# The delta rule's gates ahead of K's convolution in the program, the logits' copy on ScalarE

## The chip, the cores and the metric

One core of a Trainium2 chip. The metric is the device time of one execution in microseconds, as the median of three runs. The engines are TensorE (PE; its weight loads are PEld), VectorE (DVE), ScalarE (ACT), GpSimd (POOL) and SyncE (SP), which issues all weight transfers.

## The reference, cut to what matters

Two transformer blocks on 256 tokens of width 1024, all in float32. The first block has a mixer of two halves (retention, and a gated delta rule), a router with 32 experts of which each token uses two, and a second block follows with a pooling mixer and a convolutional feed-forward layer. What concerns the change is the delta rule's input:

```python
d_q, d_k, d_v, d_z, d_a, d_b = ...                    # columns of h @ w_in
qkv = silu(causal_dwconv(concat(d_q, d_k, d_v), conv_w))   # four taps per channel
dk = l2norm(heads(ck))
beta = sigmoid(d_b)
g = -exp(a_log) * softplus(d_a + dt_bias)             # log decay, the gate
dn = gated_delta_rule(dq, dk, heads(cv), g, beta)
```

Inside the delta rule the decay between two tokens is the exponential of differences of the running sum of g, and the matrix to be inverted is (beta k) k^T times this decay.

## The kernel before, in words

Activations are kept transposed, [128 channels x 256 tokens] per block of channels. Products in float32 are run as three matmuls on split operands (`split`, lines 281 and 284: ScalarE writes the rounded high part, VectorE or GpSimd subtracts for the low part; `mm3`, line 290: the three matmuls).

The work goes in stages: the modulation vectors from w_ada; normed and modulated input (lines 499 to 506); K's projection (line 509, into four PSUM tiles ps5); K's convolution; the gates; the matrix Am and its inverse in levels of doubling blocks (line 705, tiles Am, Zc, Xc, Q); V's and Q's convolutions; the delta rule's products; retention; the output projection; the router; 16 pairs of experts (lines 1289 and 1317); the tail with the feed-forward layer (line 290 again).

The program's order is only a rank. The framework's planner goes over all stages, and gives each engine, whenever it is free by the planner's own estimates, the ready instruction that stands first in the program. Work of a later stage so fills the waits of an earlier one. On the chip each engine's queue then runs strictly in the planned order. Only the router (TensorE, VectorE) and the experts (TensorE, SyncE) keep the order in which they are written.

The lines that the change and the prediction touch:

- `conv_silu`: line 562 scales a projection by the last tap into y, line 563 copies it raw (both ScalarE, four blocks each); line 568 adds the other three taps on VectorE, three instructions per block; line 571 is the Silu on ScalarE. For K it is called at line 600 with the ready ps5, so it issues no matmul and no DMA.
- the gates, lines 602 to 638: line 605 computes the eight logits (psab), line 608 copies them (abT), line 611 transposes them by two small matmuls, line 613 copies them out (ab). From there small operations on [128 x 8]: beta (615 to 617, an Exp and a reciprocal), xa and na (619 to 622, an Exp), and the softplus as a series on VectorE (625 to 636), up to gg at line 638.
- behind the gates: line 642 (running sum of gg by a matmul), 646 (Exp of it, egc), 651 to 661 (the decay Dm, an Exp), then `sumsq(yk)` (lines 583 to 591) and Am (685 to 689).
- `copy` (lines 205 to 210) and `affine` (lines 212 to 217) share one counter:

```python
def copy(dst, src):
    _alt[0] ^= 1
    if _alt[0]:
        V.tensor_copy(dst, src)
    else:
        S.activation(dst, src, AF.Copy)
```

  The copy of abT is the first call in the program, so it is VectorE's. Later callers are rows of the modulation (g1b, g2b), Q in the inverse, atT, rqT, rkT, rv, reto, the copies xt for the router's logits, and oT and hidT of each pair of experts.

Of the kernel before, what the change touches and what calls it, by code (L numbers as in the profile page):

```python
# [13 lines left out]
AF = mybir.ActivationFunctionType  # L14
# [6 lines left out]
T = 256  # L21
# [158 lines left out]
def build(ctx, tc, io, out, dbg=None):  # L180
    nc = tc.nc
    V, S, G, PE = nc.vector, nc.scalar, nc.gpsimd, nc.tensor
# [8 lines left out]
    def bank(tag=None):  # L191
        return pp.tile([128, 512], F32, name="ps", tag=tag or ptag[0])
# [12 lines left out]
# [6 lines that stand above are left out]
# [8 lines left out]
    def dump(name, ap):  # L219
        if dbg is not None and name in dbg:  # L220
            nc.gpsimd.dma_start(dbg[name], ap)
# [40 lines left out]
    def ft(shape, name, bufs=None, tag=None, dtype=F32):  # L262
        return fp.tile(shape, dtype, name=name, tag=tag or name, **({"bufs": bufs} if bufs else {}))

    def t4(shape, name):
        return dp.tile(shape, F32, name=name, tag="t4", bufs=N4)
# [20 lines left out]
    def mm3(ps, ah, al, bh, bl, first, last):  # L287

        for n, (a, b) in enumerate(((ah, bh), (ah, bl), (al, bh))):
            PE.matmul(ps, lhsT=a, rhs=b, start=first and n == 0, stop=last and n == 2)  # L290
# [194 lines left out]
    ps5 = [bank("pb")[:, :T] for m in range(4)]  # L485
# [43 lines left out]
    def hp(part, k, t=None):  # L529
        a = hs_[k // 4][part][:, k % 4, :]  # L530
        return a if t is None else a[:, 128 * t:128 * t + 128]
# [14 lines left out]
    def conv_silu(w, off, ps=None, first=()):  # L546

        first = list(first)
        if ps is None:
            ps = [bank("pb").rearrange("p (i t) -> p i t", i=2) for m in range(2)]  # L550
            for m in range(4):
                for k4 in range(2):
                    wh, wl = first.pop(0) if first else next(w)
                    for kk in range(4):
                        k = 4 * k4 + kk
                        mm3(ps[m // 2][:, m % 2, :], wh[:, kk, :], wl[:, kk, :], hp(0, k), hp(1, k), k == 0, k == 7)
            ps = [ps[m // 2][:, m % 2, :] for m in range(4)]
        y = t4([128, 4, T], "y")
        raw = t4([128, 4, T], "raw")
        for m in range(4):  # L560
            c = 4 * (off + m)
            S.activation(y[:, m, :], ps[m], AF.Copy, scale=convw[:, c + 3:c + 4])
            S.activation(raw[:, m, :], ps[m], AF.Copy)
        for m in range(4):
            c = 4 * (off + m)
            for tap in range(3):
                sh = 3 - tap
                V.scalar_tensor_tensor(
                    y[:, m, sh:], raw[:, m, :T - sh], convw[:, c + tap:c + tap + 1], y[:, m, sh:],
                    op0=ALU.mult, op1=ALU.add)  # L570
            S.activation(y[:, m, :], y[:, m, :], AF.Silu)
        return y
# [24 lines left out]
        G.tensor_tensor(r, x, mhalf[:, :, None].to_broadcast([128, 2, 4]), op=ALU.pow)  # L597
        return r

    yk = conv_silu(None, 4, ps5)  # L600

    psab = bank()
    for kk in range(2):
# [1 line left out]
            PE.matmul(psab[32 * q:32 * q + 32, :T], lhsT=wab[:, 2 * q + kk, :], rhs=hT(2 * q + kk),  # L605
                      start=kk == 0, stop=kk == 1)
    abT = dp.tile([128, T], F32, name="abT")
    copy(abT, psab[:, :T])
    psab2 = bank()
    for t in range(2):  # L610
        PE.matmul(psab2[:, 8 * t:8 * t + 8], lhsT=abT[:, 128 * t:128 * t + 128], rhs=cfv("sel32"), start=True, stop=True)
# [24 lines left out]
    V.scalar_tensor_tensor(xa, xa, 0.0, lnu, op0=ALU.max, op1=ALU.add)  # L636
    gg = ft([128, 2, 4], "gg")
    V.scalar_tensor_tensor(gg, xa, -1.0, ea, op0=ALU.mult, op1=ALU.mult)
    dump("gg", gg)
    dump("beta", beta)  # L640
    psg = bank()
# [899 lines left out]
```

## Time and profile before

| | us |
|---|---|
| median of three runs | 890.74 (889.5 to 893.18) |
| the profiled execution | 890.27 |
| its span, first to last instruction | 888.5 |
| TensorE busy in the span | 842.7 (95%) |
| VectorE busy | 401.4 (45%) |
| ScalarE busy | 272.4 (31%) |
| GpSimd busy | 153.1 (17%) |
| DMA, mean over the span | 288.54 MB, 325 GB/s |

Busy times are shares of the whole span, over stages with different limits; a busy TensorE may run at either level of its clock, which the granted clock shows (1.00 is full speed). In a timeline, the bracket at the end of a line is the idle time of the engine just before it and what ended it.

### The profile page before, as it was taken

What the parts mean: (1) busy time and instruction counts of PE and PEld (TensorE: products, weight loads), DVE (VectorE), ACT (ScalarE), POOL (GpSimd) and SP (SyncE); (2) the same over time, 40 slices, a digit from 0 to 9 for tenths busy, and PEclk for the clock granted to TensorE, in tenths of its full rate; (3) what the DMA queues carried; (4) which work ended last, traced back from release to release, by engine and by line L of the source; (5) the groups of instructions that cost most, each with busy time, mean ns of one, the idle gap of its engine ahead of it and who ended that gap; (6) DMA issues with size and microseconds to landing.
All of it is one profiled execution on the core that took longest, in us unless ns stands there. A gap on an engine that the chain in (4) does not pass through costs nothing.

```text
span 888.5 us, 12970 instructions
## 1 busy us (share of the span) xinstructions
PE 842.7 (95%) x5337; PEld 534.7 (60%) x5337; DVE 401.4 (45%) x757; ACT 272.4 (31%) x512; POOL 153.1 (17%) x115
## 2 busy tenths in 40 slices
PE   2988999989989999999999998998999999999998
PEld 0675778768734435343343532544435999898996
DVE  3577587586611222212122211232214977667664
ACT  2253244364501101010010100101104665555552
POOL 0234331162000000000000001021000033533525
PEclk9998999999999999999999999999999999999999
DMA  9982779767589999999999999999999955453001
GB/s 379 423 360 97 285 281 378 290 252 315 190 327 377 423 428 426 429 427 427 428 427 426 429 427 426 429 428 426 421 409 426 409 202 190 182 198 142 1 2 47
DMA packets 26113, 288.54 MB, mean 325 GB/s; under 512 B 3009, under 2 KB 3265, under 8 KB 9793
## 3 DMA queue, kind: packets, MB, share of 16 engines
q1 hardware_dynamic: 26048, 287.66, 78.6%
q8 instruction: 44, 0.72, 0.3%
q14 instruction: 21, 0.16, 0.1%
HBM read 286.60 MB, written 1.05 MB: 324 GB/s over the span
## 4 chain that ended last, share of the span: by engine, by line
PE 59%; DMA 11%; DVE 1%; issue 0%; ACT 0%; SPq 0%; DVEq 0%; ACTq 0%
PE ps L290 21%; PE ps L1289 20%; PE ps L1317 10%; DMA wt<-in_w 9%; PE ps L1225 3%; PE ps L1248 3%; DMA wt<-in_ffn_w_in 2%; PE ps L1305 1%; PE ps L1237 1%; PE ps L1235 0%; DVE x L1524 0%; DVE x L1425 0%; PE ps L1055 0%; DVE wl L284 0%; DVE hid L1298 0%
## 5 line engine op out<-in xcount | busy, mean ns | idle before, releaser
L1289 PE MATMUL ps<-wt,x 128*64 128x512 f32 x1024 | 228.3, 598 | 6.9 <-DMA wt<-in_w 5.7
L1289 PEld LDWEIGHTS ps<-wt,x 128*64 128x64 f32 x1024 | 75.2, 138 | 151.4 <-issue 134.0
L281 ACT ACTIVATE wh<-wt 128x512 fp32r<-128x512 f32 (+1 forms) x138 | 113.4, 832 | 91.1 <-PE ps L290 82.4
L1317 PE MATMUL ps<-wt,hidT 128*64 128x512 f32 x512 | 115.6, 602 | 2.9 <-issue 1.6
L284 POOL TENSOR_TENSOR wl<-wt,wh 128x512 fp32r<-128x512 f32 (+1 forms) x52 | 94.7, 1833 | 90.1 <-ACT wh L281 87.6
L1298 DVE SCALAR_TENSOR_TENSOR hid<-ps,gs,hid 128x512 f32<-128x512 f32 x16 | 12.0, 752 | 200.0 <-PE ps L1289 200.0
L290 PE MATMUL ps<-gh,wh 128*128 128x256 f32 x352 | 98.5, 280 | 0.2 <-DVE gl L1442 0.2
L290 PE MATMUL ps<-gl,wh 128*128 128x256 f32 x352 | 98.3, 280 | 0.0
L290 PE MATMUL ps<-gh,wl 128*128 128x256 f32 x352 | 98.2, 279 | 0.0
L284 DVE TENSOR_TENSOR wl<-wt,wh 128x1024 fp32r<-128x1024 f32 (+1 forms) x86 | 83.8, 987 | 31.8 <-ACT wh L281 31.6
L1317 PEld LDWEIGHTS ps<-wt,hidT 128*64 128x64 f32 x512 | 38.8, 138 | 66.6 <-issue 64.3
L1053 POOL TENSOR_TENSOR dg<-ca,csh 128x512 fp32r<-128x512 f32 x6 | 6.2, 1040 | 391.1 <-DVE csl L284 320.9
L290 PEld LDWEIGHTS ps<-gh,wh 128*128 128x128 f32 x352 | 66.0, 188 | 0.6 <-ACT gh L1440 0.4
L290 PEld LDWEIGHTS ps<-gh,wl 128*128 128x128 f32 x352 | 66.1, 188 | 0.0
L290 PEld LDWEIGHTS ps<-gl,wh 128*128 128x128 f32 x352 | 65.9, 187 | 0.2
L1328 ACT ACTIVATE Yh<-ps 128x512 fp32r<-128x512 f32 x30 | 17.9, 597 | 109.0 <-DVE ps L1326 64.3
L1326 DVE TENSOR_TENSOR ps<-ps,g2b 128x512 f32<-128x512 f32 x30 | 21.0, 700 | 60.0 <-PE ps L1317 60.0
L1499 POOL TENSOR_TENSOR yf<-yf 128x256 f32<-128x256 f32 x22 | 19.5, 886 | 164.2 <-PE ps L290 95.5
L1494 DVE SCALAR_TENSOR_TENSOR yf<-ps,sm,yf 128x254 f32<-128x254 f32 x88 | 42.0, 479 | 11.2 <-ACT yf L1491 10.0
L1294 ACT ACTIVATE hid<-ps 128x512 f32<-128x512 f32 x16 | 9.6, 597 | 107.1 <-PE ps L1289 107.1
L217 ACT ACTIVATE x<-ps,modT,A 128x256 f32<-128x256 f32 x32 | 17.8, 564 | 70.2 <-PE ps L1225 70.2
L290 PE MATMUL ps<-wh,hfl 128*128 128x512 f32 x88 | 34.7, 394 | 0.0
(388 smaller groups left out, 1268.0 us busy)
## 6 DMA issues: line engine op xcount, KB each, us to landing
wt<-in_w SPq DMA_DIRECT2D x86, 2048.0 KB, 22.1
wt<-in_w_ada SPq DMA_DIRECT2D x12, 2048.0 KB, 13.3
wt<-in_ffn_w_in SPq DMA_DIRECT2D x11, 2048.0 KB, 7.9
wt<-in_w SPq DMA_DIRECT2D x40, 512.0 KB, 10.2
wt<-in_w_in SPq DMA_DIRECT2D x7, 2048.0 KB, 13.9
wt<-in_ffn_w_out SPq DMA_DIRECT2D x5, 2048.0 KB, 8.4
wt<-in_w_out SPq DMA_DIRECT2D x2, 2048.0 KB, 7.9
wt<-in_w_in SPq DMA_DIRECT2D x2, 1024.0 KB, 19.4
```

Of the source, the lines that this page charges most:

```text
L217: S.activation(dst, src, AF.Identity, scale=a, bias=b)
L281: S.activation(hi, src, AF.Copy)
L284: (eng or V).tensor_tensor(lo, src, hi.bitcast(F32), op=ALU.subtract)
L290: PE.matmul(ps, lhsT=a, rhs=b, start=first and n == 0, stop=last and n == 2)
L1225: PE.matmul(ps[d - d % 2][:, d % 2, :], lhsT=x[:, t, 128 * d:128 * d + 128], rhs=OH[:, t].rearrange("p g s -> p (g s)"), start=t == d % 2 ...
L1248: PE.matmul(res[t, c], lhsT=oT[:, 128 * t:128 * t + 128], rhs=y, start=False, stop=False)
L1289: PE.matmul(ps[64 * g:64 * g + 64, :], lhsT=xg[:, k, 128 * (p % 2) + 64 * g:128 * (p % 2) + 64 * g + 64], rhs=wt[p, nm, g][:, k, :], start ...
L1317: PE.matmul(py[c][64 * g:64 * g + 64, :], lhsT=hidT[:, f, 64 * g:64 * g + 64], rhs=wt[p, "w2", g][:, f, 512 * c:512 * c + 512], start=f == ...
L1326: V.tensor_tensor(py[c], py[c], g2c, op=ALU.mult)
L1328: S.activation(yh, py[c], AF.Copy)
L1494: V.scalar_tensor_tensor(y[:, sh:], ps[:, :T - sh], cw[:, 3 * m + tap:3 * m + tap + 1], y[:, sh:], op0=ALU.mult, op1=ALU.add)
L1499: G.tensor_tensor(ys[0], ys[0], ys[1], op=ALU.mult)
```

## The change

The call of K's convolution moves from ahead of the gates to behind gg, and the copy of the logits, until now a call of the alternating helper, is written as a ScalarE activation. The helper's counter is therefore advanced once less, and every later call of `copy` and `affine` takes the other engine.

```diff
-    yk = conv_silu(None, 4, ps5)
 
     psab = bank()
...
     abT = dp.tile([128, T], F32, name="abT")
-    copy(abT, psab[:, :T])
+    S.activation(abT, psab[:, :T], AF.Copy)
     psab2 = bank()
...
     V.scalar_tensor_tensor(gg, xa, -1.0, ea, op0=ALU.mult, op1=ALU.mult)
+    yk = conv_silu(None, 4, ps5)
     dump("gg", gg)
```

## Rows read from the trace of the kernel before

**Rows 1.** Stretches of the span: us of stretch, busy us (instructions) by engine, granted clock, DMA share, GB/s

```profile
60.00:80.00 20.00, 18.11 (x343) 12.04 (x343) 17.96 (x44) 9.25 (x20) 9.60 (x9) 0.91 0.34 119
...
140.00:160.00 20.00, 19.95 (x92) 16.18 (x91) 13.75 (x25) 9.36 (x15) 4.04 (x4) 1.00 1.00 412
...
285.00:645.00 360.00, 352.47 (x1740) 156.19 (x1738) 84.74 (x153) 46.18 (x84) 12.55 (x12) 1.00 1.01 427
```

**Rows 2.** Chain that ended last: start us, us, what

```profile
250.79 7.09 PE ps L1289 x32
...
501.76 7.04 PE ps L1317 x32
...
508.80 36.71 DMA wt<-in_w
```

**Rows 3.** TensorE in order of time, 46 to 73 us: start, us, instruction, [idle before, releaser]

```profile
46.02 1.06 PE L605 MATMUL ps<-hT,wab 128*32 128x256 f32 x14
...
53.17 0.61 PE L611 MATMUL ps<-cf,abT 128*128 128x8 f32 x4 [2.06 <-DVE abT L208]
...
61.09 0.36 PE L642 MATMUL ps<-gg,cf 128*128 128x8 f32 x2 [0.56 <-DVE gg L638]
...
72.21 0.44 PE L705 MATMUL ps<-Zc,Am 32*32 32x16 f32 x32 [0.78 <-DVE Zc L723]
```

**Rows 4.** Stretches, line 290 (V's and Q's convolution matmuls) on TensorE alone

```profile
47.00:51.00 4.00, 3.98 (x32) 1.00 1.04 442
...
53.50:57.30 3.80, 3.66 (x18) 0.55 0.98 418
```

**Rows 5.** VectorE in order of time, 46 to 67 us

```profile
46.69 0.48 DVE L568 SCALAR_TENSOR_TENSOR y<-raw,sm,y 128x254 f32<-128x254 f32 x1
...
49.46 1.53 DVE L568 SCALAR_TENSOR_TENSOR y<-raw,sm,y 128x253 f32<-128x253 f32 x1
...
52.71 0.41 DVE L208 COPY abT<-ps 128x256 f32<-128x256 f32 x1
...
56.32 1.23 DVE L629 TENSOR_TENSOR z<-z 128x8 f32<-128x8 f32 x1
...
60.78 0.17 DVE L638 SCALAR_TENSOR_TENSOR gg<-xa,ea 128x8 f32<-128x8 f32 x1
...
66.11 0.17 DVE L591 TENSOR_SCALAR kk<-ps 128x8 f32<-128x8 f32 x1 [0.85 <-PE ps L588]
```

**Rows 6.** ScalarE in order of time, 47 to 62 us

```profile
47.06 0.43 ACT L563 ACTIVATE raw<-ps 128x256 f32<-128x256 f32 x1
...
48.06 0.42 ACT L571 ACTIVATE y<-y 128x256 f32<-128x256 f32 x1 [0.57 <-DVE y L568]
...
54.04 1.28 ACT L615 ACT_TABLE_LOAD   x1
...
55.33 0.21 ACT L615 ACTIVATE beta<-ab 128x8 f32<-128x8 f32 x1
...
61.78 0.21 ACT L646 ACTIVATE egc<-gc 128x8 f32<-128x8 f32 x1 [4.07 <-DVE gc L644]
```

**Rows 7.** GpSimd in order of time

```profile
49.40 1.30 POOL L284 TENSOR_TENSOR wl<-wt,wh 128x512 fp32r<-128x512 f32 x1 [3.03 <-ACT wh L281]
...
56.24 1.29 POOL L284 TENSOR_TENSOR wl<-wt,wh 128x512 fp32r<-128x512 f32 x1 [4.13 <-ACT wh L281]
```

**Rows 8.** Router, before the experts, 230 to 233 us, all engines

```profile
230.91 1.28 ACT L247 ACT_TABLE_LOAD   x1
...
230.94 0.69 DVE L208 COPY xt<-ps 128x512 f32<-128x512 f32 x1 [0.81 <-PE ps L1002]
...
232.20 0.29 ACT L247 ACTIVATE ss<-ss,ca 128x2 f32<-128x2 f32 x1
```

**Rows 9.** Copies by the alternating helper, lines 208 and 210: duration ns min/median/max

```profile
L208 DVE COPY hidT<-ps x16: 691/692/692, 261.0 to 668.1; 128x512 f32<-128x512 f32 x16
...
L210 ACT ACTIVATE oT<-ps x16: 383/383/384, 258.6 to 644.2; 128x256 fp32r<-128x256 f32 x16
```

## The prediction

> **What bounds the kernel now.** I read the stretches of the span first. From 285 to 645 us the DMA engines are full (share 1.01, 427 GB/s) [rows 1]: the experts' weights set the pace there, and the chain of waits agrees, since it runs over the experts' matmuls and then over weight transfers [rows 2]. That stretch can't be shortened by compute; it can only begin earlier. It begins when the stages ahead of it have released the weight buffers: from 60 to 80 us the DMA share is 0.34 [rows 1], because transfers wait for buffers. So a microsecond won before 250 us moves the experts, and then the tail, by about a microsecond.
>
> Before 250 us TensorE is the scarce engine: busy 19.95 us of 20 from 140 to 160, 18.11 from 60 to 80 [rows 1]. Its queue is in order and is filled by a plan that works on all stages at once: V's convolution matmuls, which stand far behind the gates in the program, run between the gates' small matmuls [rows 3, 4]. Hence the measure of this stage is not the chain of the gates alone, but how long TensorE stands or runs slowly in it. Three rows show that: it waits 2.06 us for abT and 0.56 us for gg, and 0.78 us for Zc in the first levels of the triangular inverse [rows 3]. After the first of these the granted clock drops: 18 matmuls of line 290 start in a stretch of 3.80 us at clock 0.55, where 32 start in 4.00 us at 1.00 [rows 4]. A matmul at full clock thus takes 4.00 / 32 = 0.125 us, 18 would take 2.25, and the loss is 1.55 us.
>
> Why abT is late: the logits are complete at 47.08 (46.02 + 1.06) [rows 3], but the copy is at 52.71 on VectorE [rows 5], behind eleven of K's twelve taps. A tap takes 0.48 us, but 1.53 where GpSimd is at a split's subtraction [rows 5, 7]. Why gg is late: a table load of 1.28 us ahead of the first Exp [rows 6], and one operation on eight columns that takes 1.23 us beside GpSimd [rows 5, 7], where its like takes 0.17 [rows 5].
>
> **The change part by part.** *The copy on ScalarE.* Its queue is free of K's eight copies at 47.49 (47.06 + 0.43) [rows 6]. A ScalarE copy of this shape takes 0.38 us [rows 9], so abT is there at 47.87 instead of 53.12 (52.71 + 0.41 [rows 5]), 5.25 us earlier. TensorE no longer waits for it: minus 2.06 us, and the slow stretch behind that wait goes with it, minus 1.55.
>
> *The gates ahead of the convolution.* Nothing is added or removed. The convolution issues no DMA and nothing on GpSimd or SyncE; eight ScalarE copies, twelve taps and four Silus are moved behind gg. Its first copies are ready before the logits, so they still begin first. What changes is rank: where a tap and a gate operation are both ready, the gate operation goes first, and taps fill the gate chain's waits, which they do at no cost as long as VectorE has waits to fill. Behind the waiting gate operations on VectorE stand the remaining taps, and for these wait K's Silus, the squares and the sums of squares; the sums are read by VectorE at 66.11 now [rows 5].
>
> *The new wait.* The plan now puts the matmul of gg earlier into TensorE's queue, and whatever makes gg late against the plan becomes a wait there, with V's matmuls queued behind it. The present wait of 0.56 is only what remains after TensorE itself had been slowed by 1.55, so gg is about 2.11 us late against the plan. The same two causes give 1.28 for the table load and 1.23 minus 0.17 = 1.06 for the collision: 2.34 us. That is the wait I put at gg, in place of 0.56. Its bounds: 0 if the taps fill it and TensorE has V's matmuls queued in front, and 4.90 if two more table loads get into the chain (2.34 + 2 x 1.28). I take 2.34, being the two rows' own sum. The slow clock after it costs between 0 and 1.55; a wait of 2.06 was followed by it, one of 0.56 was not [rows 3, 4], and I take half, 0.78. The wait for Zc (0.78) has V's matmuls nearly used up ahead of it; with the levels starting earlier more of them remain as filler. Bounds 0 and 0.78; I take it as gone.
>
> *Table loads.* The rows show one load between K's Silus and the gates' Exps [rows 6]. With the gates' Exps ahead of most Silus the queue goes Silu, Exp, Silu, Exp: three loads, two more than now, 2.57 us on ScalarE. ScalarE stands idle 4.07 us before egc [rows 6], which covers them if the Silus do not come between the gates' two Exps. Without that cover each one between them costs 1.28.
>
> Here a rule speaks against the change. The row shows a load of 1.28 us from 54.04 and the next Exp at 55.33 [rows 6], with nothing in between. The Trainium skill (ScalarE: Activation LUTs, What ACT_TABLE_LOAD costs) counts about 2.66 us for each switch of a set, as a drain of about 1.38 goes with the load. By it the wait at gg would be 3.72 and the sum 1.38 us higher than mine; the trace shows no drain, so I keep the row's figure.
>
> *The alternation.* The helper that alternates copies between the two engines is called once less, so every later pair of calls swaps engines. Most swaps cancel (one goes each way). Two do not. hidT goes to ScalarE and oT to VectorE for the experts: 0.69 us against 0.38 for half the width [rows 9], inside a stretch bound by DMA, so nothing. And the last logits' copy ahead of the router (0.69 us on VectorE at 230.94) moves into ScalarE's queue, ahead of the table load that starts at 230.91 and lets the square root run at 232.20 [rows 8]. That adds between 0 and 0.69; I take 0.6, since the root waits for the load there.
>
> The sum: minus 2.06, 0.56, 1.55 and 0.78, plus 2.34, 0.78 and 0.6, is minus 1.2 us. The profiled execution took 890.27 us around its span of 888.5, 0.47 under the median shown; carried to the median, 890.74 - 1.2 = 889.5.
>
> **The rivals.** *The gate chain sets the stage, not TensorE's total.* Then the 5.25 us of abT count, less one switch of 1.28 in front of the Exps, and the 0.85 us that VectorE waits for the sums of squares [rows 5] go too: 5.25 - 1.28 + 0.85 - 0.6 = 4.2 earlier, 886.5. For it: the levels do wait for this chain. Against: TensorE has other work queued almost all the time.
>
> *Exps and Silus take turns, slower.* If a Silu of K gets between the gates' two Exps, the chain to gg holds three loads in place of one; TensorE waits 4.90 instead of 2.34 at gg's matmul and the slow stretch is had in full: plus 2.57 and 0.77 on my sum, 892.8. It decides from the point where the wait at gg exceeds the 4.17 that go now (2.06 + 0.56 + 1.55). For it: the Silu at 48.06 [rows 6] stands right where the first Exp becomes ready. Against: gates now rank first. The Trainium skill (same page, Rules for kernel authors) asks to do all of one set before switching; with its price per switch this case would be 4.1 us later still, 896.9.
>
> *The change doesn't do what it says:* the copy or the gates are still planned behind the taps, or kk2 becomes the last input in place of gg (it is 0.85 late already [rows 5]). Then 890.7.
>
> **How the numbers follow.** I give my forecast 0.42, the chain 0.25, the turns 0.20 and no effect 0.13. The range reaches from the chain's time with no wait at gg to the turns with a swap or two more against it: 885.0 to 894.0. A measurement of this kernel can tell about 0.5% (4.45 us; the three runs span 0.4%). Faster by more needs under 886.3: half of the chain's chance and a little of the forecast's, 0.19. Slower needs over 895.2: a third of the turns' chance, by dearer switches, and some for an unlucky order further on, 0.13. The rest, 0.68, is within.
>
> **What would show it.** Right: abT on ScalarE before 48.5 us, no wait on TensorE at line 611, two to three table loads where there was one, a wait of 2 to 3 us at line 642, gg before 58 us, and the first matmul of line 1289 about a microsecond earlier. The chain is right if the gate matmul waits are gone and the levels begin 4 us earlier with that gain kept at the experts. The turns show as four or more table loads before 62 us and a longer wait at line 642. I am wrong in kind if the difference arises behind 100 us, in the swapped copies or the weight loads.

## The result and the profile after the change

The changed kernel takes 901.74 us (median of four runs, 900.98 to 902.31) against 891.82 for the kernel before in the same session: a ratio of 1.0113, with a 95% interval from 1.0089 to 1.0137. It is slower by some 10 us, outside the forecast's range. Its profiled execution took 902.31 us around a span of 900.5, 12.0 us longer than that of the kernel before.

The chain of waits shows on which side of the experts this arises (start us, us, what):

```profile
262.72 7.09 PE ps L1289 x32
...
520.07 36.98 DMA wt<-in_w
```

The first piece at line 1289 comes 11.9 us later than in [rows 2], so the time is lost ahead of it, and what is lost there is kept to the end. The stretches that answer to [rows 1] agree (the columns are the same):

```profile
60.00:80.00 20.00, 18.17 (x279) 13.26 (x283) 14.81 (x37) 6.61 (x13) 8.19 (x7) 0.76 0.28 105
...
285.00:645.00 360.00, 353.25 (x1741) 152.44 (x1738) 77.61 (x148) 48.06 (x82) 12.09 (x12) 1.00 1.01 427
```

In the experts the pace is the same, 427 GB/s in both. From 60 to 80 us TensorE is as busy as before, but with 279 matmuls in place of 343, at a granted clock of 0.76 where it was 0.91.

TensorE's waits from 44 to 260 us (engine, line, what it waited for: us in total, times, longest) name two places:

```profile
PE ps L642 <- DVE gg L637: 4.8, 1, 4.8
PE ps L976 <- DVE dno L945: 3.0, 1, 3.0
...
PE ps L290 <- DVE wl L284: 1.9, 1, 1.9
PE ps L1016 <- DVE router L1094: 0.9, 1, 0.9
PE ps L705 <- DVE Zc L723: 0.8, 1, 0.8
```

The kernel before has these in their place, beside the waits of [rows 3]:

```profile
PE ps L290 <- DVE wl L284: 2.2, 2, 2.0
...
PE ps L976 <- DVE modT L411: 1.8, 1, 1.8
```

The first place is in the stage that was changed; the second is some 150 us later, in the stage that gates the two branches' outputs, where the diff touches nothing.

*The first place.* TensorE in order of time, the answer to [rows 3] (start, us, instruction, idle before and releaser):

```profile
48.94 0.51 PE L610 MATMUL ps<-cf,abT 128*128 128x8 f32 x4
...
55.37 0.28 PE L290 MATMUL ps<-hh,wh 128*128 128x256 f32 x1
60.49 0.57 PE L642 MATMUL ps<-gg,cf 128*128 128x8 f32 x2 [4.84 <-DVE gg L637]
```

The wait for abT is gone. In its place stands one wait of 4.84 us for gg. (In this execution the logits' matmuls start 0.99 us later than in [rows 3], at 47.01; a shift of this size in the times below says nothing of the change.) ScalarE (to be held against [rows 6]):

```profile
48.13 0.39 ACT L607 ACTIVATE abT<-ps 128x256 f32<-128x256 f32 x1
...
50.77 1.28 ACT L614 ACT_TABLE_LOAD   x1
52.06 0.21 ACT L614 ACTIVATE beta<-ab 128x8 f32<-128x8 f32 x1
...
52.39 1.28 ACT L571 ACT_TABLE_LOAD   x1
53.69 1.03 ACT L571 ACTIVATE y<-y 128x256 f32<-128x256 f32 x3
54.62 1.65 ACT L281 ACTIVATE wh<-wt 128x512 fp32r<-128x512 f32 x3
56.30 1.28 ACT L646 ACT_TABLE_LOAD   x1
```

abT comes from ScalarE at 48.13, as forecast, and there are three table loads, as forecast. But look at what stands behind the second: three Silus, and then three of the splits' high parts (line 281) in a row. No idle time stands in front of them, so what they read was there already, and they stood behind the loads and the Silus in this in-order queue. In the kernel before, the two of this stretch came one by one:

```profile
55.55 0.61 ACT L281 ACTIVATE wh<-wt 128x512 fp32r<-128x512 f32 x1
57.08 0.63 ACT L281 ACTIVATE wh<-wt 128x512 fp32r<-128x512 f32 x1 [0.92 <-PE ps L290]
```

GpSimd makes the low parts from them, and so it gets three at once, where [rows 7] has them apart:

```profile
55.32 3.71 POOL L284 TENSOR_TENSOR wl<-wt,wh 128x512 fp32r<-128x512 f32 x3 [3.00 <-ACT wh L281]
```

VectorE's gate series runs exactly beside it, the answer to [rows 5]:

```profile
49.66 0.17 DVE L612 COPY ab<-ps 128x16 f32<-128x16 f32 x1
...
54.55 4.50 DVE L632 SCALAR_TENSOR_TENSOR lnu<-lnu,z 128x8 f32<-128x8 f32 x7
...
60.17 0.17 DVE L637 SCALAR_TENSOR_TENSOR gg<-xa,ea 128x8 f32<-128x8 f32 x1
...
68.53 0.17 DVE L591 TENSOR_SCALAR kk<-ps 128x8 f32<-128x8 f32 x1 [1.32 <-PE ps L588]
```

The logits' sums are read at 49.66, and still gg is no earlier than 60.17: seven operations on eight columns each take 4.50 us together. What they take undisturbed is shown by e8 below, 1.37. In the kernel before they took 2.35, beside one subtraction on GpSimd:

```profile
57.79 2.35 DVE L633 SCALAR_TENSOR_TENSOR lnu<-lnu,z 128x8 f32<-128x8 f32 x7
```

*The second place* comes up with the experiments that reach it, since it has to be told apart from the first.

*The router*, the answer to [rows 8]: the last copy of the logits now stands on ScalarE, with the table load right behind it.

```profile
242.16 0.60 ACT L210 ACTIVATE xt<-ps 128x512 f32<-128x512 f32 x1
242.78 1.28 ACT L247 ACT_TABLE_LOAD   x1
```

### The profile page after: what moved, and what is told of

Read it like the earlier page. It is cut to its first block, busy times and chain, and to the rows that moved or that the text cites. A ratio compares the mean times of both kernels' runs of the same rounds, so it can differ in the third digit from the quotient of the medians.

```text
span 900.5 us, 12963 instructions
## 1 busy us (share of the span) xinstructions
PE 850.6 (94%) x5337; PEld 535.0 (59%) x5337; DVE 393.6 (44%) x756; ACT 278.3 (31%) x515; POOL 148.8 (17%) x115
## 4 chain that ended last, share of the span: by engine, by line
PE 58%; DMA 11%; DVE 1%; ACT 1%; issue 0%; SPq 0%; DVEq 0%; ACTq 0%
PE ps L290 20%; PE ps L1289 20%; PE ps L1317 10%; DMA wt<-in_w 9%; PE ps L1225 3%; PE ps L1248 3%; DMA wt<-in_ffn_w_in 2%; PE ps L1305 1%; ACT hidT L210 0%; DVE x L1524 0%; PE ps L1237 0%; DVE x L1425 0%; PE ps L1235 0%; PE ps L1055 0%; DVE wl L284 0%
## 5 line engine op out<-in xcount | busy, mean ns | idle before, releaser
L1289 PEld LDWEIGHTS ps<-wt,x 128*64 128x64 f32 x1024 | 73.0, 138 | 154.3 <-issue 135.5
L284 DVE TENSOR_TENSOR wl<-wt,wh 128x1024 fp32r<-128x1024 f32 (+1 forms) x86 | 81.6, 961 | 36.1 <-ACT wh L281 35.8
L1326 DVE TENSOR_TENSOR ps<-ps,g2b 128x512 f32<-128x512 f32 x30 | 21.0, 700 | 60.9 <-PE ps L1317 60.8
L210 ACT ACTIVATE hidT<-ps 128x512 f32<-128x512 f32 x16 | 9.5, 597 | 102.4 <-PE ps L1305 102.4
L382 PE MATMUL ps<-wt,srep 128*32 128x512 f32 x160 | 26.7, 810 | 11.5 <-DMA wt<-in_w_ada 11.5
```

The source lines that it names most:

```text
L284: (eng or V).tensor_tensor(lo, src, hi.bitcast(F32), op=ALU.subtract)
L382: PE.matmul(ps[32 * q:32 * q + 32, :], lhsT=srep[:, 2 * q + kk, :], rhs=w[:, 2 * q + kk, :], start=kk == 0, stop=kk == 1)
L1289: PE.matmul(ps[64 * g:64 * g + 64, :], lhsT=xg[:, k, 128 * (p % 2) + 64 * g:128 * (p % 2) + 64 * g + 64], rhs=wt[p, nm, g][:, k, :], start ...
L1326: V.tensor_tensor(py[c], py[c], g2c, op=ALU.mult)
```

## The experiments

The diff has three effects: the convolution moves behind the gates; the copy of abT goes to ScalarE; and every later copy changes its engine, because the helper's counter advances once less. The first four runs make these one by one. In the table, times are medians, ratios are against the kernel before in the same session, and the events are starts in us in the profiled execution: gg, the first rqT, the second reto, the router's logits. The last column is the distance from the second reto to the router. The events are those of one execution each, and the executions already differ by up to 1.4 us where the logits' matmuls start (45.63 in e8, 47.03 in e10); the ratios decide, the events only show the place.

| kernel | us | ratio (95%) | gg | rqT | reto | router | reto to router |
|---|---|---|---|---|---|---|---|
| before | | 1 | 60.8 | 141.9 | 178.4 | 232.7 | 54.3 |
| after | 901.74 | 1.0113 (1.0089 to 1.0137) | 60.2 | 148.0 | 185.2 | 244.7 | 59.5 |
| e1 | 896.94 | 1.0058 (1.0041 to 1.0075) | 61.3 | 141.9 | 179.1 | 238.0 | 58.9 |
| e2 | 895.22 | 1.0038 (1.0018 to 1.0058) | 59.2 | 146.9 | 183.3 | 238.4 | 55.1 |
| e3 | 895.24 | 1.0038 (1.0024 to 1.0053) | 59.8 | 150.4 | 186.4 | 238.5 | 52.1 |
| e4 | 899.63 | 1.0089 (1.0071 to 1.0106) | 62.7 | 153.6 | 190.6 | 243.3 | 52.7 |
| e5 | 897.05 | 1.0062 (1.0042 to 1.0083) | 59.2 | 146.9 | 184.2 | 239.9 | 55.7 |
| e6 | 893.11 | 1.0028 (1.0013 to 1.0044) | 60.5 | 144.0 | 181.3 | 236.5 | 55.2 |
| e7 | 885.33 | 0.9936 (0.9917 to 0.9956) | 57.2 | 137.4 | 173.9 | 229.0 | 55.1 |
| e8 | 885.64 | 0.9942 (0.9921 to 0.9963) | 57.3 | 138.8 | 175.3 | 228.8 | 53.5 |
| e9 | 886.47 | 0.9948 (0.9922 to 0.9973) | 56.3 | 136.9 | 174.2 | 229.4 | 55.2 |
| e10 | 897.63 | 1.0087 (1.0058 to 1.0117) | 61.7 | 152.2 | 189.3 | 240.9 | 51.6 |

**e1, the swapped copies alone** (edit of the kernel before):

```diff
-    copy(abT, psab[:, :T])
+    V.tensor_copy(abT, psab[:, :T])
```

> Only the alternation is changed: the gates stay behind K's convolution, the logits' copy stays on VectorE, but no longer advances the counter, so every later copy swaps engines as in the changed kernel. Theory G (the loss of some 11 us arises in the gates' stage): within 1 us of the kernel before, first expert matmul after the branch near 251 us. Theory S (the swapped copies further on cost it): 5 us or more slower, with the loss behind 180 us, and both stages up to 100 us as before.

Measured: 1.0058. The swaps that the forecast took for nearly free cost about 5 us. The place is the last column: 58.9 us from reto to the router, 4.6 more than before, and 59.5 in the changed kernel.

**e2, the move and the copy without the swaps** (edit of the changed kernel):

```diff
-    S.activation(abT, psab[:, :T], AF.Copy)
+    S.activation(abT, psab[:, :T], AF.Copy); _alt[0] ^= 1
```

> The whole change, but the counter is advanced once by hand, so that every later copy is on the engine it had before. Theory G: slower than before by 7 to 11 us, with the wait of some 4.8 us for gg and the late levels as in the changed kernel. Theory S: within 2 us of before, or slower by no more than the 2.4 us that the levels begin later in the changed kernel. Both at work: 5 to 7 us slower.

Measured: 1.0038, some 3.4 us, between what theory S allowed (2.4) and the 5 to 7 us expected if both are at work, and the distance from reto to the router is back at 55.1. The loss lies in front: rqT is 5.0 us late. The wait for gg is there in full (4.83 us), and so are the seven operations of 4.50 us. So the change holds two separate losses, and by e1 and e2 they add: 0.0058 + 0.0038 = 0.0096 of the time, inside the interval of the whole change (0.0089 to 0.0137).

**e3, the move alone; e4, the copy alone** (edits of the changed kernel and of the kernel before):

```diff
-    S.activation(abT, psab[:, :T], AF.Copy)
+    copy(abT, psab[:, :T])
```

```diff
-    copy(abT, psab[:, :T])
+    S.activation(abT, psab[:, :T], AF.Copy); _alt[0] ^= 1
```

> Only the move: the gates ahead of K's convolution, the copy on VectorE by the alternating helper as before (no swap later on). Theory G, with the move as the cause: slower by 5 us or more. If instead the copy's engine is what puts gg's matmul too early in TensorE's queue: within 2 us of before. Theory S: within 2 us.

> Only the copy on ScalarE, with the counter advanced by hand (no swap) and the gates still behind K's convolution. Theory G, with the move as the cause: within 2 us of before, or 2 to 3 us faster, since the wait of 2.06 us for abT goes. If the copy's engine is the cause: slower by 3 us or more. Theory S: within 2 us.

Measured: 1.0038 and 1.0089. The move alone costs what the move and the copy cost together, and has the same mark: four subtractions in a row on GpSimd, the seven operations at 4.55 us beside them, and a wait of 4.2 us at line 642. So the engine of the copy isn't what makes gg late in the changed kernel. The copy alone is slower than both together, so the two parts don't add. In e4 a Silu does come between the gates' two Exps, with a table load on either side of it (at 53.37 and 55.10), and VectorE waits for the second Exp:

```profile
56.63 0.17 DVE L625 TENSOR_SCALAR z<-na 128x8 f32<-128x8 f32 x1 [2.81 <-ACT na L622]
```

That is the forecast's rival of the turns, in a kernel for which it was not made; gg is at 62.7 here, the latest of all in the table. But this is the smaller part of the loss of e4; for the rest e10 and e11 were made.

**e5 and e6, one row copy put back.** With the swaps, VectorE's order in the gated stage differs. In e1 (start, us, instruction, idle before):

```profile
189.72 0.69 DVE L944 TENSOR_TENSOR dno<-dno,dsq 128x512 f32<-128x512 f32 x1 [1.75 <-POOL dsq L253]
190.34 2.49 DVE L284 TENSOR_TENSOR wl<-wt,wh 128x512 fp32r<-128x512 f32 x4
```

and in the kernel before:

```profile
188.55 2.49 DVE L284 TENSOR_TENSOR wl<-wt,wh 128x512 fp32r<-128x512 f32 x4
192.57 0.69 DVE L944 TENSOR_TENSOR dno<-dno,dsq 128x512 f32<-128x512 f32 x1 [1.53 <-POOL dsq L253]
```

A product of the delta rule's norm, which has to wait for GpSimd's power, has got ahead of the four subtractions for which TensorE's last gated projection waits. One copy was suspected, beside the other swaps: the row of the modulation with j = 11, the second half of g2b (it has nothing to do with K). Both edits put that copy back on VectorE, e5 in the changed kernel, e6 in e1:

```diff
-        copy(dst, ps)
+        _alt[0] ^= j == 11; copy(dst, ps); _alt[0] ^= j == 11
```

> The whole change, with one of the swapped copies (the row of the modulation for K's eleventh block) put back on VectorE; every other copy stays swapped. Theory of one copy: it alone, beside the other swaps, makes VectorE's plan put the product of the delta rule's norm (line 945) ahead of the four splits' subtractions (line 284) in the gated stage. Then the splits come first again, the wait of TensorE at line 290 in that stage (1.9 to 2.0 us) and the half clock behind it go, the stretch from reto to the router falls from 59.5 to about 54 us, and the time is about 897 (896 to 898). Rival, many small swaps: the stretch stays over 58 us and the time stays at 901 to 902.

> The kernel before with all later copies swapped, as in e1_flip_only, but with the same one copy put back on VectorE. Theory of one copy: the 5 us that e1_flip_only cost go, time 891.5 to 893, stretch from reto to the router about 54 us. Rival, many small swaps: 896 to 897 as in e1_flip_only.

Measured: 1.0062 and 1.0028, with the distance from reto to the router at 55.7 and 55.2. In e5 VectorE makes the subtractions first again, and TensorE's wait at line 976 is shorter and for another thing (2.99 us for dno in the changed kernel):

```profile
194.16 1.89 DVE L284 TENSOR_TENSOR wl<-wt,wh 128x512 fp32r<-128x512 f32 x3
...
197.57 0.69 DVE L944 TENSOR_TENSOR dno<-dno,dsq 128x512 f32<-128x512 f32 x1 [0.66 <-POOL dsq L253]
```

```profile
206.17 0.63 PE L976 MATMUL ps<-ca,dno 128*128 128x128 f32 x4 [1.28 <-DVE modT L411]
```

So one swapped copy of 512 columns, beside the other swaps, is worth 3.7 to 3.8 us in that stage (59.5 - 55.7, 58.9 - 55.2); by the ratios of the whole time it is 4.5 us in one pair and 2.7 in the other. What it costs with no other copy swapped was not run. One detail was expected wrongly: the wait at line 290 stays (2.00 us in e5); it is 2.05 in the kernel before as well and never belonged to the loss.

e6 is still 0.0028 above the kernel before, some 2.5 us. At the router 0.8 of it is seen: TensorE waits 0.94 us at line 1016 in every kernel with the swaps, 0.16 without. The rest shows in front in this execution, where rqT is 2.1 us later than in the kernel before. But e1, with the same order on VectorE, ScalarE and GpSimd up to 110 us, has rqT at 141.9, as the kernel before has, so a cause for this rest isn't shown: two executions of the same order differ by as much.

**e7 and e8, fewer subtractions beside the gates.** Half of V's splits (the row blocks 2 and 3) are subtracted on VectorE instead of GpSimd, in e2 and in the kernel before:

```diff
-    def conv_splits(w):
+    def conv_splits(w, pool=CPOOL):
...
-                            G if m in CPOOL else V)
+                            G if m in pool else V)
 
-    v_splits = conv_splits(w_in[6])
+    v_splits = conv_splits(w_in[6], (0, 1))
```

> The move and the copy without the swaps, as in e2_change_no_flip, but half of V's split subtractions (the row blocks 2 and 3) go from GpSimd to VectorE. Theory of the collision: TensorE's wait of 4.83 us at line 642 is the gates' series on VectorE (4.50 us where 1.4 would do) beside GpSimd's subtractions; with fewer of these beside it gg is 2 to 3 us earlier, the wait falls to 2.5 or less, and the time is 1 to 4 us under that of e2_change_no_flip, so 891 to 894. Rival, the table loads and ScalarE's queue make gg late: the wait stays over 4 us, the time at 895 or above.

> The kernel before with the same half of V's split subtractions on VectorE: the control for e7_splits_shared. Theory of the collision: the gates' operations in the kernel before lie only partly beside GpSimd (one of 1.23 us), so the gain here is at most 1 us: 891 to 893. Rival, GpSimd is the general limit of this stage: the kernel before gains as much as e7_splits_shared does, 888 to 890.

Measured: 0.9936 and 0.9942. e7 is 0.0102 of the time faster than e2, some 9 us and more than was expected, and the wait at line 642 is gone. VectorE in e7, where GpSimd does nothing between 47.9 and 63.4 us:

```profile
53.52 1.18 DVE L632 SCALAR_TENSOR_TENSOR lnu<-lnu,z 128x8 f32<-128x8 f32 x6
...
57.24 0.17 DVE L637 SCALAR_TENSOR_TENSOR gg<-xa,ea 128x8 f32<-128x8 f32 x1
```

and in e8 the whole series:

```profile
55.24 1.37 DVE L633 SCALAR_TENSOR_TENSOR lnu<-lnu,z 128x8 f32<-128x8 f32 x7
```

ScalarE's three table loads are still there in e7, at 50.37, 51.99 and 55.90 us; they aren't the cause of the wait. What ended it are two things that these runs don't part further. gg comes 2.0 us earlier (57.24 against 59.19; 2.5 if the later start of that execution is taken off, abT at 47.74 against 47.15). And the low parts are ready sooner, so the plan puts 17 more matmuls of line 290 ahead of gg's: at 0.12 us each 2.0 us. Together 4.5 of the 4.83.

The stretches of e2 and e7 show what else went with the wait (columns as in [rows 1]). e2:

```profile
55.00:60.00 5.00, 0.50 (x3) 0.53 (x3) 4.76 (x8) 1.57 (x2) 3.93 (x4) 0.70 0.90 342
60.00:70.00 10.00, 10.00 (x77) 8.09 (x80) 5.61 (x15) 4.82 (x11) 2.49 (x3) 0.81 0.44 187
70.00:85.00 15.00, 13.73 (x396) 7.23 (x392) 10.87 (x29) 2.77 (x5) 5.69 (x5) 0.77 0.31 115
```

e7:

```profile
55.00:60.00 5.00, 4.88 (x33) 3.89 (x31) 4.08 (x13) 2.55 (x6) 0.00 (x0) 1.00 1.00 403
60.00:70.00 10.00, 9.32 (x189) 8.31 (x187) 8.36 (x19) 6.96 (x16) 6.51 (x6) 1.00 0.37 156
70.00:85.00 15.00, 12.29 (x366) 6.35 (x368) 12.32 (x33) 3.95 (x7) 4.37 (x4) 0.79 0.38 143
```

After TensorE has stood, the granted clock is 0.81 for the next 10 us, and a loss of 10 x 0.19 = 1.9 us follows; without the wait it is 1.00. From 70 to 85 us the clock is low in both (0.77 and 0.79), so that isn't the wait's doing.

The control moves too: the kernel before gains 0.0058. So its own stage lay beside GpSimd more than was expected (at most 1 us was): in e8 the first eleven taps take 5.11 us where they took 7.17 before, abT starts at 50.25, and TensorE waits neither for it nor for gg. The rival of e8, that GpSimd limits this stage in general, is thus right in part. But the gain of e7 over e2 is 0.0102, and with the collision out of both, the move and the copy cost nothing that the intervals show (0.9936 against 0.9942). e7 and e8 also beat both kernels of this case.

**e9, both repairs in the whole change** (the edits of e5 and e7):

> The whole change with both repairs: the row copy back on VectorE as in e5_row_copy_put_back, half of V's split subtractions on VectorE as in e7_splits_shared. If the two causes are all, they add: e7_splits_shared came out 0.0102 of the time under e2_change_no_flip, and e5_row_copy_put_back lies at 1.0062, so 0.996 of the time before, 886 to 888 us, gg before 58 us, no wait of TensorE at line 642, and 54 to 56 us from reto to the router. Rival, a third cause that belongs to the whole change alone (a transfer or a copy in another place): 891 us or more.

Measured: 0.9948, gg at 56.3, no wait at line 642, 55.2 us from reto to the router. The kernel to hold this against is e8, which has the shared splits without the change: 0.9942. So the two causes found account for the loss of the change; a third one beyond the intervals' 2 to 3 us doesn't show.

**e10, the copy alone with shared splits; e11, transfers in the inverse.** e10 is the edits of e4 and e7 together. e11 adds to the kernel before, after the third level of the inverse:

```diff
-        ada("L%d" % lev)
+        (lev != 2) or (V.tensor_copy(g2b[:, 0:4], Zc[:, 0, :, 31]), [nc.gpsimd.dma_start(g2b.rearrange("p (k n) -> p k n", k=2), io["w_in"][0][:, 0:2, :]) for i in range(8)]); ada("L%d" % lev)
```

> The copy on ScalarE alone, without the move and the swaps, as in e4_copy_only, with half of V's split subtractions on VectorE. If the collision in the gates' stage is what started the loss of e4_copy_only, the time is that of e8_before_splits_shared, 885 to 887 us, and TensorE's waits at line 705 that no releaser explains total 2 to 3 us. Rival, the loss belongs to the inverse's stage itself (weights of w_in transferred 8 us earlier beside it): those waits total 6 us or more again and the time is 891 or more.

> The kernel before with 4 MB of transfers added in the middle of the triangular inverse (eight loads of 512 KB into a buffer that nothing reads before it is overwritten, started by the third level's result); every engine's order is otherwise that of the kernel before. e4_copy_only and e10_copy_only_splits_shared had 8.1 and 8.4 us of TensorE waits at line 705 without a releaser, in a stretch in which weights of w_in were in transfer; the kernel before has 2.5 there, with the DMA engines at 4 GB/s. Theory of the transfers: with traffic in this stretch those waits grow to 6 us or more and the time goes up by 3 to 8 us, to 894 to 899. Rival, the order of TensorE's instructions in the copy-only kernels: the waits stay at 2 to 3.5 us and the time within 2 us of before.

Measured: e10 1.0087, as slow as e4, so the loss of the copy alone is not the collision in the gates. Most of it lies in the inverse: at the wait for Zc in the first levels e4 is 3.3 us behind the kernel before and e10 1.6, at the first rqT 11.7 and 10.3. TensorE in e4 waits there three times with nothing that the profile shows as a releaser:

```profile
88.73 0.83 PE L705 MATMUL ps<-Zc,Am 32*32 32x16 f32 x46 [2.22 <-issue]
95.42 0.71 PE L705 MATMUL ps<-Zc,Am 32*32 32x16 f32 x63 [1.07 <-issue]
102.16 0.28 PE L705 MATMUL ps<-Q,Xc 32*32 32x16 f32 x2 [4.84 <-issue]
```

The kernel before has one such wait:

```profile
85.75 0.71 PE L705 MATMUL ps<-Zc,Am 32*32 32x16 f32 x34 [2.49 <-issue]
```

e11 took 911.45 us (1.0246, 1.0205 to 1.0288), but it doesn't decide what it was made for. The added loads waited for one another, so that from 88 to 92 us only 94 GB/s moved, and their issues blocked GpSimd's queue, with the splits' subtractions behind them:

```profile
89.52 0.55 POOL L726 DMA_DIRECT2D g2b<-in_w_in  x1 [4.26 <-DMA g2b<-in_w_in]
```

The time is lost behind that: rqT comes at 162.7. The one wait without a releaser was 2.74 us, with 315 GB/s moving from 84 to 88 us; it did not grow. Why the copy alone makes three of them stays open. For the change itself it matters little: the changed kernel has one, of 2.90 us.

## Why the prediction was wrong

*What bounds the kernel* was right: the changed kernel is 11.9 us late at 262 us and 12.0 at the end, so what is lost ahead of the experts is lost at the end. TensorE's waits and its slow stretches ahead of the experts were the right measure.

*The waits that go* were right. abT is on ScalarE at 48.13, nothing waits at line 610, and the slow stretch behind that wait is gone: TensorE is busy 9.66 us of 10 from 45 to 55 us in e2, at clock 1.00. The wait for Zc, taken as gone, stayed at 0.78; its other bound was the true one.

*The new wait* is the first step that failed: 2.34 us forecast, 4.84 measured, at the upper bound of 4.90 though not for that bound's reason, so that the bound held by luck. Of its two causes the collision with GpSimd was the right one, and it was sized too small: one operation, 1.06 us, because one such operation showed in [rows 5]. A second stood in the same trace, the seven operations at 2.35 us, 0.98 more than undisturbed. And the change moved the whole gate series to where GpSimd has three subtractions in a row: the seven operations alone lose 4.50 - 1.37 = 3.13 us, and one close behind them (line 634, beside GpSimd's memset) took 0.66 where e8 has 0.17. With the 1.28 of the first table load this makes 1.28 + 3.13 + 0.49 = 4.90; but that the load is part of the wait isn't shown, since e7 has the same load ahead of the Exp and no wait. The forecast knew the price of one collision and didn't ask how many there would be. For that, ScalarE's queue had to be followed one step on: two more table loads and three Silus ahead of the high parts (line 281) hold these back and release them together. The forecast called ScalarE's idle time cover for the loads, and it was, for ScalarE; for those who wait for its high parts it wasn't.

The Trainium skill (SBUF — State Buffer, Who interferes with whom and Summary: rules for kernel authors) says that a VectorE instruction with two inputs in SBUF and a GpSimd instruction that reads SBUF exclude each other for a whole instruction: the second one blocks until the first is done. The trace agrees: three subtractions of about 1.24 us (3.71 / 3), and a series that comes out 3.13 us longer. It is the rule that should have been weighed here: read so, a collision is priced by the number of GpSimd instructions and their length, and not by VectorE's.

*The slow clock* behind the wait was put at 0.78, with 1.55 as upper bound. In e2 it is 1.9 us, over that bound (0.81 for 10 us, where the kernel before has 1.00 from 60 to 70 us): this term was too small as well. The sum of this stage, mended: - 2.06 - 0.56 - 1.55 + 4.83 + 1.9 = + 2.6 us, beside a measured + 3.4 for e2 (0.0038 of 892; 1.6 to 5.2). With the 3.7 and 0.8 of the swaps below it is 7.1 of the 10 us that were lost; the rest has no place that the runs show.

*The table loads* came as forecast, three. The row again shows the Exp 0.01 us behind the load (50.77 + 1.28, then 52.06), so the drain that the Trainium skill counts for a switch (ScalarE: Activation LUTs, What ACT_TABLE_LOAD costs) isn't seen here either; that its higher price was nearer to the measured wait is chance. The rival in which Exps and Silus take turns had the right sign, but no Silu came between the gates' two Exps (52.06 and the next at 52.18), and e7 keeps the three loads and has no wait; only e4 and e10 had the turns.

*The alternation* is the second step that failed. "Most swaps cancel (one goes each way). Two do not" counts copies by their duration. The two that were named came as forecast: hidT on ScalarE costs nothing in the experts, and the last copy ahead of the router costs 0.8 us where 0.6 was taken. But the order on each engine is planned with these durations, and a third copy, which itself is on no critical path, changed VectorE's order some 15 us later: 3.7 to 3.8 us. No row of the kernel before shows that; what could have been known is that a swap of every later copy has a plan of its own as an effect, with a cost on both sides of zero, and the range had no term for it. The text named the sign of being wrong in kind, a difference behind 100 us in the swapped copies. The swaps are about half of the loss (0.0058 of 0.0113, by e1).

## What to carry to other kernels

When a step moves, price what it will run beside, not what it runs beside now: count the instructions of the other engine that will be there, and follow what a longer queue holds back and then releases in a bunch. A helper that alternates engines makes a small edit into a change of everything behind it; pin the engine, or keep the counter's parity, before judging the edit. And repair the collision first: with half of the subtractions elsewhere both orders gain, and the order that was in question makes no difference; the copy alone, without the move, still loses (e10).

## What the runs showed of the hardware

Which engine pays for a collision is not fixed by the order of instructions on each engine. In the kernel before, the eleven taps took 7.17 us and the two subtractions beside them 2.71; in e6 the same instructions in the same order took 5.12 and 3.90:

```profile
45.62 7.17 DVE L568 SCALAR_TENSOR_TENSOR y<-raw,sm,y 128x253 f32<-128x253 f32 x11 [1.60 <-ACT raw L563]
...
49.40 2.71 POOL L284 TENSOR_TENSOR wl<-wt,wh 128x512 fp32r<-128x512 f32 x2 [3.03 <-ACT wh L281]
```

```profile
45.77 5.12 DVE L568 SCALAR_TENSOR_TENSOR y<-raw,sm,y 128x253 f32<-128x253 f32 x11 [1.60 <-ACT raw L563]
...
49.56 3.90 POOL L284 TENSOR_TENSOR wl<-wt,wh 128x512 fp32r<-128x512 f32 x2 [3.02 <-ACT wh L281]
```

Both outcomes come again: 7.17 and 2.71 in e11, 5.11 and 3.89 in e1. The starts don't tell them apart either: in both the first subtraction starts 0.06 us ahead of a tap (49.40 and 49.46; 49.56 and 49.62). In the first case that tap then takes 1.53 us, in the second the subtraction takes 2.46. In e6, as in e1, abT was then in time, but three later operations of the gates lay beside GpSimd (1.07, 1.24 and 2.09 us), gg was hardly earlier (60.52 against 60.78), and TensorE, which got there sooner, had one wait of 3.69 us in place of 2.06 and 0.56.

TensorE's waits without a releaser in the inverse (up to 5.4 us, in e10) weren't in the forecast at all. Instructions come by a DMA queue of their own, 44 packets in the changed kernel, of 16 KB each:

```profile
q8 instruction: 44, 0.72, 0.3%
```

That such a wait is one for instructions fits the place, many tiny matmuls in a row, but no run here shows it.
